# A two-block transformer on one core: second products' weights fetched and split earlier, more first products ahead of the gates, and layer 0's second product turned to sums by feature

## The chip, the cores and the metric

The kernel runs on one core of one Trainium2 chip. The metric is the device time of one execution in microseconds, and of several executions the median is compared. A core has five engines that run their own instruction streams in order and wait for one another by semaphores: TensorE (PE in the profile, with its weight loads as PEld), VectorE (DVE), ScalarE (ACT), GpSimd (POOL) and SyncE (SP). SP, POOL and ACT also issue DMAs.

## The reference, cut to what matters

The program is a block of two attention layers on 256 tokens of 1024 features, and behind it a second block with two layers. Each layer of the second block ends in a feed-forward part that chooses 16 of 16384 experts for each token and each of 8 heads:

```
def peer_ffn(x, w_q, sub_keys, u_emb, v_emb):
    ...
        q = (xc @ w_q).reshape(PEER_CHUNK, PEER_HEADS, 2, PEER_HALF)
        s = jnp.einsum('thid,hikd->thik', q, sub_keys).astype(jnp.float32)
        s1, i1 = lax.top_k(s[:, :, 0], PEER_TOPK)
        s2, i2 = lax.top_k(s[:, :, 1], PEER_TOPK)
        ...
        top_s, pos = lax.top_k(cand, PEER_TOPK)
        eidx = jnp.take_along_axis(cidx, pos, axis=-1)
        gate = jax.nn.softmax(top_s, axis=-1)
        u = u_emb[eidx]
        hid = jax.nn.gelu(jnp.einsum('td,thkd->thk', xc, u))
        wgt = (gate * hid.astype(jnp.float32)).astype(xc.dtype)
        return jnp.einsum('thk,thkd->td', wgt, v_emb[eidx])
```

Layer 0 does this for two sets of 256 tokens (`x` and a context), layer 1 for `x` alone.

## The kernel before, in words

For the tokens of `x` the kernel does not gather the chosen experts. It goes over all 16384 experts in 128 chunks of 128, and multiplies by a gate that is zero where an expert was not chosen. This is `peer`, which runs once in each layer.

For chunk j, `hid(j)` is the **first product**: the chunk's rows of `peer_u` times the tokens, then a gelu. It has two forms. The first `nnat` chunks go in plain float32 (`mm1`, L436, 8 matmuls, each in two records of the profile). The others go as three products of halves (`mm3`, L429 to L431, 24 matmuls): each weight chunk is split into a rounded part `wa` (ACT, L295) and a remainder `wb` (DVE, L297). `wgt(j)` loads four chunks of gates (`gp`, SP, L1629), multiplies the gelu by them (DVE, L1632) and splits the result into `W` (ACT L1634, DVE L1635). `vside(j)` is the **second product**: `W` times the chunk's rows of `peer_v`, summed over all chunks in four PSUM banks. In layer 0 (`NT` is 256) the stationary operand is a piece of `W` for 128 tokens and the chunk of `peer_v` streams by in 512 columns: 12 matmuls, sums by token (L1659 to L1661). In layer 1 (`NT` is `TD`, 224 tokens) a 128 by 128 piece of `peer_v` is stationary and `W` streams by: 24 matmuls of 224 columns, sums by feature (L1651 to L1653). The other 32 tokens of layer 1 are done by gathered rows (`rows_x`), as is the whole context of layer 0 (`rows`, 512 gathered rows of 512 KB, on POOL and DVE).

The first `npre` first products stand ahead of the loop, with their results in `gpre` tiles. `ffn_start` mixes them with two pieces of work: `topk`, the choice of the experts (products with `peer_wq` and the keys on PE, L436 and L1289, then a long run of small DVE instructions, and transposes, L1410), and `gbuild`, which builds the gates (DVE L1576 and L1578, PE L1553, ACT L1557) and writes them to DRAM (`G`, issued from ACT, L1564). `lead` advances a side generator by a rate for each unit of the main one, `par` shares by weights, and `until(pe)` runs `peer` up to its `yield None`. In layer 0, `topk` goes with `lead` at rate `EARLY[0]` after `SOLO` steps of its own, and `gbuild` goes with `par`. In layer 1, `topk` and `gbuild` are one chain and go with `par` against the first products.

Weights come through `WS`: `load` issues 512 KB DMAs on SP in the order of the code, `split` makes `wa` and `wb`, and `get` keeps `depth` loads and `lead` splits ahead. All large tiles share one pool of 42 buffers. The order on PE is that of the code up to the end of layer 0's `ffn_start`; behind that, and on the other engines, a scheduler sets the order when the program is built. While `peer` of layer 0 runs, `along` advances `rows` by `RATE[3]` rows for each unit that it yields.

The main loop of `peer` takes 130 steps, each with `hid(j)` where j is `npre` or more, `wgt(j - 1)` and `vside(j - 2)`.

## Time and profile before

| | us |
|---|---|
| median of 3 runs (3629.66 to 3637.85) | 3633.35 |
| the profiled execution | 3631.59 |
| its span, first to last instruction | 3629.5 |

| engine | busy, share of the span |
|---|---|
| PE | 88% |
| PEld | 80% |
| DVE | 77% |
| ACT | 41% |
| POOL | 26% |

The span is the time from the first to the last instruction. A matmul's duration overlaps its neighbours', so the distance between starts says more than the duration. In layer 0 the first matmul of the second product starts 1519.27 us into the span, in layer 1 at 3010.7; all that is told below of places goes by these times. A number in brackets behind a row is how long the engine stood idle before it, and what ended that.

### The profile page before, as it was taken

The page shows a single profiled execution, that of the slowest core. Times are in us where ns is not written, and L with a number is a line of the kernel's source. Part 1 is how long each engine was busy: PE and PEld are TensorE (multiplying, and loading weights), DVE is VectorE, ACT ScalarE, POOL GpSimd, SP SyncE. Part 2 cuts the span into 40 slices and gives each one's busy share as a digit, 9 for nine tenths or more (in the row PEclk, how much of TensorE's full clock was granted, in tenths as well). Part 3 has the DMA queues.
Part 4 walks back from the last instruction along what each step waited for, and adds up shares of the span by engine and source line. Part 5 has one row for each costly group of instructions (what it writes and reads, how often), then busy time and mean ns, then how long its engine had stood idle before and what let it go on. Part 6 is the DMA issues. An engine that isn't in the chain of part 4 may idle for free. (4 is left out here: it accounts for less than half of the span.)

```text
span 3629.5 us, 60668 instructions
## 1 busy us (share of the span) xinstructions
PE 3205.7 (88%) x23160; PEld 2911.8 (80%) x23160; DVE 2780.5 (77%) x5718; ACT 1484.5 (41%) x2788; POOL 936.3 (26%) x831
## 2 busy tenths in 40 slices
PE   7989999878699788679999999768999689999999
PEld 5877999657598777558888888658888589999999
DVE  4375675877899799899889899797575968777655
ACT  3454444314355203424434344334362154444444
POOL 2002112123234301475555555251000003111000
PEclk9989999988799899789999999879999799999999
DMA  8537457657688937999999999775444099888764
GB/s 308 163 123 281 159 162 266 211 208 261 226 280 314 343 123 226 324 419 393 379 369 383 371 387 390 239 278 185 134 126 171 25 295 350 298 284 289 259 217 151
DMA packets 315427, 941.06 MB, mean 259 GB/s; under 512 B 29616, under 2 KB 93136, under 8 KB 315136
## 3 DMA queue, kind: packets, MB, share of 16 engines
q1 hardware_dynamic: 130848, 468.77, 36.3%
q0 software_dynamic: 118816, 432.76, 33.0%
q10 hardware_dynamic: 65472, 35.66, 3.3%
q8 instruction: 181, 2.97, 0.3%
q14 instruction: 110, 0.90, 0.1%
HBM read 893.01 MB, written 43.02 MB: 258 GB/s over the span
## 5 line engine op out<-in xcount | busy, mean ns | idle before, releaser
L297 DVE TENSOR_TENSOR wb<-wr,wa 128x1024 fp32r<-128x1024 f32 x842 | 1010.3, 1222 | 289.8 <-ACT wa L295 267.2
L295 ACT CAST wa<-wr 128x1024 fp32r<-128x1024 f32 x842 | 852.1, 1046 | 87.2 <-DMA wr<-in_w 27.4
L429 PE MATMUL pu<-hnh,wa 128*128 128x256 f32 x2000 | 585.9, 293 | 23.1 <-ACT wa L295 22.7
L431 PE MATMUL pu<-hnh,wb 128*128 128x256 f32 x2000 | 582.0, 291 | 23.2 <-DVE wb L297 23.0
L430 PE MATMUL pu<-hnl,wa 128*128 128x256 f32 x2000 | 579.3, 290 | 1.6 <-DVE hnl L559 1.6
L1447 POOL DMA_INDIRECT row<-in_pu,ridx x256 | 357.4, 1396 | 516.6 <-DVE wb L297 92.3
L429 PE MATMUL pu<-xh,wa 128*128 128x256 f32 (+1 forms) x1728 | 484.1, 280 | 0.9 <-ACT xh L1618 0.9
L430 PE MATMUL pu<-xl,wa 128*128 128x256 f32 (+1 forms) x1728 | 483.3, 280 | 1.5 <-DVE xl L1619 1.5
L1447 POOL DMA_INDIRECT row<-in_pv,ridx x256 | 362.6, 1417 | 466.4 <-DVE wb L297 113.3
L431 PE MATMUL pu<-xh,wb 128*128 128x256 f32 (+1 forms) x1728 | 482.8, 280 | 0.0
L429 PEld LDWEIGHTS pu<-hnh,wa 128*128 128x128 f32 x2000 | 397.3, 199 | 37.5 <-ACT wa L295 25.7
L431 PEld LDWEIGHTS pu<-hnh,wb 128*128 128x128 f32 x2000 | 396.8, 198 | 30.9 <-DVE wb L297 29.2
L430 PEld LDWEIGHTS pu<-hnl,wa 128*128 128x128 f32 x2000 | 397.3, 199 | 2.6 <-DVE hnl L559 2.1
L429 PEld LDWEIGHTS pu<-xh,wa 128*128 128x128 f32 x1728 | 333.3, 193 | 10.3 <-ACT wa L295 4.3
L430 PEld LDWEIGHTS pu<-xl,wa 128*128 128x128 f32 x1728 | 333.2, 193 | 5.2 <-DVE xl L1619 1.8
L431 PEld LDWEIGHTS pu<-xh,wb 128*128 128x128 f32 x1728 | 332.5, 192 | 1.6 <-issue 0.4
L436 PE MATMUL pu<-xn,wr 128*128 128x256 f32 (+1 forms) x1408 | 325.8, 390 | 4.4 <-ACT xn L573 4.4
L1469 DVE SCALAR_TENSOR_TENSOR racc<-row,rwg,racc 128x1024 f32<-128x1024 f32 x254 | 325.9, 1283 | 0.4
L1459 DVE CUSTOM_DVE_ANT_0 row<-row,xr 128x1024 f32<-128x1024 f32 x256 | 311.0, 1221 | 5.6 <-issue 5.2
L436 PEld LDWEIGHTS pu<-xn,wr 128*128 128x128 f32 x1408 | 276.3, 200 | 44.9 <-issue 7.5
L1609 ACT ACTIVATE gel<-pu 128x256 f32<-128x256 f32 (+1 forms) x204 | 75.7, 371 | 566.6 <-PE pu L431 532.6
L1651 PE MATMUL pm<-W,wa 128*128 128x224 f32 x1024 | 276.0, 275 | 1.6 <-ACT wa L295 1.6
(430 smaller groups left out, 6395.3 us busy)
## 6 DMA issues: line engine op xcount, KB each, us to landing
wr<-in_w SPq DMA_DIRECT2D x288, 512.0 KB
wr<-in_pu SPq DMA_DIRECT2D x256, 512.0 KB
wr<-in_pv SPq DMA_DIRECT2D x256, 512.0 KB
wr<-in_w POOLq DMA_DIRECT2D x130, 512.0 KB
wm<-in_wmod POOLq DMA_DIRECT2D x96, 512.0 KB
G<-gt ACTq DMA_DIRECT2D x60, 512.0 KB
gp<-G SPq DMA_DIRECT2D x32, 512.0 KB
gp<-G SPq DMA_DIRECT2D x32, 448.0 KB
```

Of the source, the lines that this page charges most:

```text
L295: nc.scalar.copy(a, r)
L297: nc.vector.tensor_tensor(b, r, a, op=OP.subtract)
L429: mm(out, ah, bh, start=i == 0, stop=False)
L430: mm(out, ah, bl, start=False, stop=False)
L431: mm(out, al, bh, start=False, stop=i == n - 1)
L436: s.nc.tensor.matmul(out, w[:, k * 128:(k + 1) * 128], x(k), start=k == 0, stop=k == 7)
L1447: nc.gpsimd.indirect_dma_start(out=t, out_offset=None, in_=tab[w], in_offset=bass.IndirectOffsetOnAxis(ap=s.ridx[:, tt, i:i + 1], axis=0))
L1459: v.tensor_tensor_reduce(t, t, xr[tt], 1.0, 0.0, OP.mult, OP.add, hid[:, i:i + 1])
L1469: v.scalar_tensor_tensor(out[tt], t, wg[:, i:i + 1], out[tt], op0=OP.mult, op1=OP.add)
L1609: nc.scalar.activation(g, bank[:, :NT], AF.Gelu_apprx_tanh)
L1651: mm(o, vh[:, c], W[:, 0], start=j == 0 and d % 2 == 0, stop=False, skip_group_check=True)
```

## The change

- `NPRE` goes from (20, 24) and (20, 28) to (20, 28) and (24, 36): layer 0 has 28 first products ahead of the loop, 20 of them plain; layer 1 has 36, 24 of them plain.
- Layer 1's `ffn_start` is now built as layer 0's: `lead` during `topk` (rate 4.0), `par` with `gbuild` (64 to 75). Layer 0's weight in `par` goes from 50 to 60.
- `peer` loads four chunks of `peer_v` and splits two before its `yield None`, that is before the first gates are loaded.
- The second product of layer 0 takes the form of layer 1's, with 256 columns, and its sums by feature are added to `h` in place; the copies (L1690), the transposes and the additions by 128 columns of `add_ffn` (L1532, L1535) are left out for `x`.

```diff
-NPRE = (20, 24), (20, 28)
-
-EARLY = 6.0, 50.0
+NPRE = (20, 28), (24, 36)
+
+EARLY = (6.0, 60.0), (4.0, 75.0)
...
             hid(j)
             yield NT / (75 if j < nnat else 100)
+
+        wv.load(DV + 2)
+        wv.split(2)
         yield None
...
         def vside(j):
             vh, vl = wv.get()
             W = Wt.pop(j)
-            if NT < T:
-                for d in range(8):
...
-                return
-            for tt in range(NT // 128):
-                wh, wl = W[:, 0, tt * 128:(tt + 1) * 128], W[:, 1, tt * 128:(tt + 1) * 128]
-                for dh in range(2):
-                    c, bank = slice(dh * 512, dh * 512 + 512), acc[tt, dh]
-                    mm(bank, wh, vh[:, c], start=j == 0, stop=False)
-                    mm(bank, wh, vl[:, c], start=False, stop=False)
-                    mm(bank, wl, vh[:, c], start=False, stop=j == 127)
+            for d in range(8):
+                c = slice(d * 128, (d + 1) * 128)
+                o = acc[d // 4, d // 2 % 2][:, d % 2 * T:d % 2 * T + NT]
+
+                mm(o, vh[:, c], W[:, 0], start=j == 0 and d % 2 == 0, stop=False, skip_group_check=True)
+                mm(o, vh[:, c], W[:, 1], start=False, stop=False, skip_group_check=True)
+                mm(o, vl[:, c], W[:, 0], start=False, stop=j == 127, skip_group_check=True)
...
         h = s.h_load(s.hd["x"], eng)
+        m5 = s.mod(l, 0, 5)
+        for d in range(8):
+            x = h.ch(d)[:, :NT]
+            v.scalar_tensor_tensor(x, acc[d // 4, d // 2 % 2][:, d % 2 * T:d % 2 * T + NT], m5(d), x,
+                                   op0=OP.mult, op1=OP.add)
         if NT < T:
...
-        for tt in range(2 if NT == T else 0):
-            evs = []
-            for dh in range(2):
-                evs.append(s.s2([128, 512], "pev"))
-                nc.scalar.copy(evs[-1], acc[tt, dh])
-            s.add_ffn(h, l, 0, tt, evs)
...
-    tk = k.topk(l, rx["xn"], ws, eng, rx, skew=bool(early))
+    tk = k.topk(l, rx["xn"], ws, eng, rx, skew=l == 0)
...
-    if not early:
-        gb = lambda: k.gbuild(rx, G, k.nc.scalar, ntc, skew=False)
-        yield from par(k, (chain(tk, gb), TG), (pre, tot))
-        return
     yield from lead(tk, (pre, early))
-    yield from par(k, (k.gbuild(rx, G, k.nc.scalar, ntc), 64.0), (pre, tot))
+    yield from par(k, (k.gbuild(rx, G, k.nc.scalar, ntc, skew=l == 0), 64.0), (pre, tot))
...
-        drain(along(ffn_start(k, 0, rx, ws, k.G[0], pe, *EARLY), rows, RATE[2]))
+        drain(along(ffn_start(k, 0, rx, ws, k.G[0], pe, *EARLY[0]), rows, RATE[2]))
...
-    drain(ffn_start(k, 1, rx, ws, k.G[1], pe, None, NPRE[1][1] * 2.99, ntc=TD // 32))
+    drain(ffn_start(k, 1, rx, ws, k.G[1], pe, *EARLY[1], ntc=TD // 32))
```

Three places show how the instructions move. The first is SP's queue in layer 0, where the first gates `gp` are loaded; `in_pu` and `in_pv` are the tables of the first and the second product. Before:

```order
L282 DMA wr_14648<-in_pu 128x1024
L282 DMA wr_14758<-in_pu 128x1024
L1629 DMA gp_15043<-G_98 128x1024
L282 DMA wr_15059<-in_pv 128x1024
L282 DMA wr_15061<-in_pv 128x1024
L282 DMA wr_15063<-in_pv 128x1024
L282 DMA wr_15097<-in_pv 128x1024
L282 DMA wr_15128<-in_pv 128x1024
L1629 DMA gp_15152<-G_98 128x1024
```

The same place of SP's queue with the change:

```order
L282 DMA wr_15018<-in_pv 128x1024
L282 DMA wr_15020<-in_pv 128x1024
L282 DMA wr_15022<-in_pv 128x1024
L282 DMA wr_15024<-in_pv 128x1024
L1631 DMA gp_15194<-G_98 128x1024
L282 DMA wr_15287<-in_pv 128x1024
L1631 DMA gp_15323<-G_98 128x1024
```

Four of the five chunks of `peer_v` that stood behind the first gates now stand ahead of them, and one is left behind them.

The second place is PE in layer 1, right behind the last products with the keys (L1289) of `topk`, up to the transposes L1410 that wait for the choices; each pair of L436 rows on one `pu` is one first product. Before:

```order
L436 MATMUL pu_27848<-xn_27035,wr_27701 128x224 x3
L436 MATMUL pu_27905<-xn_27034,wr_27734 128x224 x4
L436 MATMUL pu_27905<-xn_27035,wr_27734 128x224 x4
L1410 MATMUL pm_27763<-ct,tt_27764 128x128
L1410 MATMUL pm_27763<-ct,tt_27767 128x128
L1410 MATMUL pm_27763<-ct,tt_27770 128x128
```

The same place on PE with the change:

```order
L436 MATMUL pu_29231<-xn_28532,wr_29198 128x224 x3
L436 MATMUL pu_29250<-xn_28531,wr_29210 128x224 x4
L436 MATMUL pu_29250<-xn_28532,wr_29210 128x224 x4
L436 MATMUL pu_29263<-xn_28531,wr_29229 128x224 x4
L436 MATMUL pu_29263<-xn_28532,wr_29229 128x224 x4
L436 MATMUL pu_29282<-xn_28531,wr_29248 128x224 x4
L436 MATMUL pu_29282<-xn_28532,wr_29248 128x224 x4
L436 MATMUL pu_29337<-xn_28531,wr_29261 128x224 x4
L436 MATMUL pu_29337<-xn_28532,wr_29261 128x224 x4
L436 MATMUL pu_29374<-xn_28531,wr_29280 128x224 x4
L436 MATMUL pu_29374<-xn_28532,wr_29280 128x224 x4
L1410 MATMUL pm_29309<-ct,tt_29310 128x128
```

Five whole first products stand there instead of one, so four more. One more stands between the six transposes and the first gate matmul (L1553), where before there was none.

The third place is PE in layer 0's main loop: one second product, `pm` being the four banks of sums. Before, the whole of it:

```order
L1659 MATMUL pm_15033<-wa_18007,W_18002 128x512
L1660 MATMUL pm_15033<-wb_18008,W_18002 128x512
L1661 MATMUL pm_15033<-wa_18007,W_18002 128x512
L1659 MATMUL pm_15034<-wa_18007,W_18002 128x512
L1660 MATMUL pm_15034<-wb_18008,W_18002 128x512
L1661 MATMUL pm_15034<-wa_18007,W_18002 128x512
L1659 MATMUL pm_15035<-wa_18007,W_18002 128x512
L1660 MATMUL pm_15035<-wb_18008,W_18002 128x512
L1661 MATMUL pm_15035<-wa_18007,W_18002 128x512
L1659 MATMUL pm_15036<-wa_18007,W_18002 128x512
L1660 MATMUL pm_15036<-wb_18008,W_18002 128x512
L1661 MATMUL pm_15036<-wa_18007,W_18002 128x512
```

With the change, the first half of one:

```order
L1652 MATMUL pm_15184<-W_19818,wa_19823 128x256
L1653 MATMUL pm_15184<-W_19818,wa_19823 128x256
L1654 MATMUL pm_15184<-W_19818,wb_19824 128x256
L1652 MATMUL pm_15184<-W_19818,wa_19823 128x256
L1653 MATMUL pm_15184<-W_19818,wa_19823 128x256
L1654 MATMUL pm_15184<-W_19818,wb_19824 128x256
L1652 MATMUL pm_15185<-W_19818,wa_19823 128x256
L1653 MATMUL pm_15185<-W_19818,wa_19823 128x256
L1654 MATMUL pm_15185<-W_19818,wb_19824 128x256
L1652 MATMUL pm_15185<-W_19818,wa_19823 128x256
L1653 MATMUL pm_15185<-W_19818,wa_19823 128x256
L1654 MATMUL pm_15185<-W_19818,wb_19824 128x256
```

It goes on in the same way for the two other banks: 24 matmuls of 256 columns stand for 12 of 512.

## Rows read from the trace of the kernel before

**Rows 1.** Busy time by stretch: us, busy us (instructions), clock share, DMA share, GB/s

```profile
core 0: us, PE busy (x) PEld busy (x) DVE busy (x) ACT busy (x) POOL busy (x), PEclk, DMA share, GB/s
1440.00:1519.00 79.00, 40.96 (x364) 36.68 (x362) 60.73 (x91) 33.54 (x145) 25.62 (x20) 0.71 0.90 285
1519.00:1631.00 112.00, 85.90 (x337) 66.57 (x337) 110.29 (x156) 34.03 (x54) 80.11 (x53) 0.87 1.03 419
1631.00:2272.00 641.00, 594.49 (x3660) 532.85 (x3661) 583.16 (x770) 267.29 (x416) 343.33 (x236) 0.98 0.99 382
2852.00:2885.00 33.00, 1.80 (x6) 1.19 (x7) 31.26 (x169) 4.73 (x14) 0.00 (x0) 0.56 0.00 0
2885.00:2976.00 91.00, 79.46 (x681) 75.59 (x681) 69.61 (x111) 45.88 (x237) 0.00 (x0) 0.88 0.78 240
```

**Rows 2.** The same view for L1660 alone, four to a second product

```profile
1519.00:1631.00 112.00, 42.43 (x96) 20.56 (x96) 0.87 1.03 419
1631.00:2272.00 641.00, 168.45 (x412) 81.35 (x412) 0.98 0.99 382
```

**Rows 3.** Timeline of PE, layer 0's main loop: start, us, instruction [idle before]

```profile
1719.19 0.28 PE L431 MATMUL pu<-xh,wb 128*128 128x256 f32 x1
1719.31 0.40 PE L1659 MATMUL pm<-wa,W 128*128 128x512 f32 x1
1719.54 0.40 PE L1660 MATMUL pm<-wb,W 128*128 128x512 f32 x1
...
1724.93 0.40 PE L1659 MATMUL pm<-wa,W 128*128 128x512 f32 x1
...
1732.41 1.20 PE L1659 MATMUL pm<-wa,W 128*128 128x512 f32 x4 [1.71 <-ACT wa L295]
```

**Rows 4.** Waits by pair: us in total, times, longest

```profile
PE pm L1659 <- ACT wa L295: 85.6, 32, 17.1
```

**Rows 5.** Timeline of ACT ahead of such a wait

```profile
1706.17 0.38 ACT L1609 ACTIVATE gel<-pu 128x256 f32<-128x256 f32 x1 [5.23 <-PE pu L430]
...
1706.74 1.99 ACT L295 CAST wa<-wr 128x1024 fp32r<-128x1024 f32 x2
```

**Rows 6.** Timeline of SP, DVE and PE where layer 0's second products begin

```profile
1506.71 0.33 SPq L1629 DMA_DIRECT2D gp<-G  x1
1507.15 5.35 SPq L282 DMA_DIRECT2D wr<-in_pv  x5
...
1515.40 1.43 DVE L1632 TENSOR_TENSOR gpre<-gpre,gp 128x256 f32<-128x256 f32 x4 [8.09 <-DMA gp<-G]
...
1519.27 2.08 PE L1659 MATMUL pm<-wa,W 128*128 128x512 f32 x4 [17.14 <-ACT wa L295]
```

**Rows 7.** Timeline of PE in layer 1, end of the choices

```profile
2847.64 4.33 PE L436 MATMUL pu<-xn,wr 128*128 128x224 f32 x22
2874.37 0.47 PE L1410 MATMUL pm<-ct,tt 128*128 128x128 f32 x1 [22.41 <-ACT tt L1409]
2881.63 1.33 PE L1410 MATMUL pm<-ct,tt 128*128 128x128 f32 x5 [6.79 <-ACT tt L1409]
2885.38 0.37 PE L1553 MATMUL pm<-gat,hot 128*128 128x128 f16 x2 [2.42 <-DVE gat L1578]
```

**Rows 8.** Timeline of ACT in layer 1's main loop, two steps in a row

```profile
3201.43 0.36 ACT L1609 ACTIVATE gel<-pu 128x224 f32<-128x224 f32 x1 [2.26 <-PE pu L431]
...
3206.79 0.36 ACT L1609 ACTIVATE gel<-pu 128x224 f32<-128x224 f32 x1 [2.27 <-PE pu L431]
```

**Rows 9.** Groups by line, of the page: the remainders of split weights

```profile
L297 DVE TENSOR_TENSOR wb<-wr,wa 128x1024 fp32r<-128x1024 f32 x842 | 1010.3, 1222 | 289.8 <-ACT wa L295 267.2
```

**Rows 10.** End of layer 0's additions (timeline), and a 256-column addition's group

```profile
2276.57 4.23 DVE L1535 SCALAR_TENSOR_TENSOR h<-pu,modT,h 128x128 f32<-128x128 f32 x16
...
L1266 DVE SCALAR_TENSOR_TENSOR h<-pu,modT,h 128x256 f32<-128x256 f32 x24 | 10.6, 480 | 31.8 <-PE pu L431 27.0 <-issue 4.9
```

**Rows 11.** Timeline of SP and DVE in layer 1, the first gates

```profile
2986.19 0.33 SPq L1629 DMA_DIRECT2D gp<-G  x1
...
3004.13 1.29 DVE L1632 TENSOR_TENSOR gpre<-gpre,gp 128x224 f32<-128x224 f32 x4
```

More of the change, by code (lines that the diff above doesn't have):

```diff
@@ L1645, in vside @@
             W = Wt.pop(j)
-            if NT < T:
-                for d in range(8):
-                    c = slice(d * 128, (d + 1) * 128)
-                    o = acc[d // 4, d // 2 % 2][:, d % 2 * T:d % 2 * T + NT]
-                    mm(o, vh[:, c], W[:, 0], start=j == 0 and d % 2 == 0, stop=False, skip_group_check=True)
-                    mm(o, vh[:, c], W[:, 1], start=False, stop=False, skip_group_check=True)
-                    mm(o, vl[:, c], W[:, 0], start=False, stop=j == 127, skip_group_check=True)
-                return
-            for tt in range(NT // 128):
-                wh, wl = W[:, 0, tt * 128:(tt + 1) * 128], W[:, 1, tt * 128:(tt + 1) * 128]
-                for dh in range(2):
-                    c, bank = slice(dh * 512, dh * 512 + 512), acc[tt, dh]
-                    mm(bank, wh, vh[:, c], start=j == 0, stop=False)
-                    mm(bank, wh, vl[:, c], start=False, stop=False)
-                    mm(bank, wl, vh[:, c], start=False, stop=j == 127)
+            for d in range(8):
[4 more added lines that the diff above has]
+                mm(o, vl[:, c], W[:, 0], start=False, stop=j == 127, skip_group_check=True)
         for j in range(130):
@@ L1672, in peer @@
         h = s.h_load(s.hd["x"], eng)
+        m5 = s.mod(l, 0, 5)
[3 more added lines that the diff above has]
+                                   op0=OP.mult, op1=OP.add)
         if NT < T:
             rows = rows()
-            m5 = s.mod(l, 0, 5)
-            for d in range(8):
-                x = h.ch(d)[:, :NT]
-                v.scalar_tensor_tensor(x, acc[d // 4, d // 2 % 2][:, d % 2 * T:d % 2 * T + NT], m5(d), x,
-                                       op0=OP.mult, op1=OP.add)
             bank = s.ps("u")
```

## The prediction

> **What bounds the kernel now.** I read the busy time by stretch first, to see which engine is full where the change falls, then the timelines of PE and of its releasers at four places. Layer 0's feed-forward part has two regimes [rows 1, 2]. From 1519 to 1631 us 96 records of L1660 make 24 second products, almost all without a first product beside them: 112.0 / 24 = 4.67 us a step. DVE is busy for 110.3 of the 112 us and PE for 85.9, so DVE (with the gathered rows of the context) and the DMAs (share 1.03) set the pace. From 1631 to 2272 there are 412 / 4 = 103 steps of 641 / 103 = 6.22 us, with a first product in nearly all. PE is busy for 594.5 of 641 us there, DVE for 583.2: PE is the bound, with waits. The reader is to see in [rows 3] what a step is made of. Matmuls of 256 columns start 0.12 us apart, matmuls of 512 columns 0.23, and two second products in a row start 1724.93 - 1719.31 = 5.62 apart, PE full. But at 1732.41 PE stood for 1.71 us until ACT had rounded a weight chunk. Without the first of them such waits are 31, of 68.5 us in total [rows 4]. ACT is not slow there, it is in line: its gelu waited for the first product to end, and the rounding stands behind the gelu [rows 5]. At 1502 PE fell idle for 17.14 us, up to the first second product [rows 6].
>
> In layer 1 PE is full in the main loop: ACT's gelu waits for PE at each step, and the steps are 3206.79 - 3201.43 = 5.36 us long [rows 8], 48 matmuls of 0.112 us, so 2.68 for a first and 2.68 for a second product. What PE loses there it loses at the end of the choices: between 2851.97 and 2885.38 it waits 22.41 + 6.79 + 2.42 = 31.6 us for DVE's selection and what hangs on it [rows 7], with DVE busy for 31.3 of 33 us and no DMA running [rows 1].
>
> **The change part by part.** The sum is made against the profiled execution's 3631.59 us (span 3629.5 and 2.1 around it); it stands 1.76 below the median of the runs, 3633.35.
>
> *Layer 0's second product turned.* 12 matmuls of 512 columns go, 24 of 256 come. The new form takes 24 x 0.12 = 2.88 us. The old one took 5.62 - 2.88 = 2.74, the first product beside it being 24 matmuls of 256 columns too [rows 3]. That is 0.14 us more a step. In the 100 steps with a first product PE is the bound and it counts: +14. The wait for ACT does not shrink, for it hangs on the end of the first product and not on the second. In the 28 steps without one, DVE covers it; if that cover is gone it costs 28 x 0.14 = 4 more. From the other side, PE's waits (641 - 594.5 = 46.5 us) could take all of it in, and then it costs nothing. Bounds 0 to +18; I take +14, the rows being from the same loop.
>
> [...]
>
> *Four more first products beside layer 0's gates.* Four steps go at 4.67 instead of 6.22: -6.2. Their four remainders on DVE, 1.22 us each [rows 9], now fall into the building of the gates: 4.9 us, where DVE idled 79 - 60.7 = 18.3 us between 1440 and 1519 [rows 1]. Half of it hides, I say: +2.5. Together -3.7, with bounds of -6.2 (all hidden) and -1.3 (none).
>
> *Weights of the second product ahead of the gates, layer 0.* Before, the first gates were issued at 1506.71 and multiplied at 1515.40, while five chunks of `peer_v` were issued right behind them on the same queue; PE began at 1519.27, when the first chunk was rounded [rows 6]. Now four chunks are loaded and two split by then. From the multiplication to PE were 3.9 us. The multiplication, the rounding and the remainder of W stay in that path, some 1.5 us by the 0.36 us of one multiplication [rows 6]: -2.4. The gates' flight of 8.7 us no longer shares the engines with five chunks: between 0 and 5 x 0.524 MB at 419 GB/s [rows 1] = -6.3, and I take -2, since row gathers stay in flight. Together -4.4, bounds -8.7 and 0. What is late next is the gates themselves, which neither edit hastens. SP's queue has nothing else behind the four loads but the gates' load, and that waits for G anyway.
>
> *End of layer 0.* Four copies, 16 transposes and 16 additions of 128 columns go; the additions alone took 4.23 us [rows 10]. Eight additions of 0.48 come, straight from the banks, the first ones before the last bank is complete. The additions alone give 4.23 - 8 x 0.48 = -0.4; if they hide altogether, -4.2. I take -3.
>
> Layer 0: +14 - 3.7 - 4.4 - 3 = +2.9.
>
> *Layer 1's first products into the choices.* The order shows five more of them ahead of the first gate matmul, four before the transposes and one behind. One is 16 records at 4.33 / 22 = 0.197 us [rows 7], 3.15 us; five fill 15.7 of the 31.6 idle us. In all eight more stand ahead of the loop, four of them plain, 4 x 3.15 + 4 x 2.68 = 23.3 us. So 23.3 - 15.7 = 7.6 us are left over for the building of the gates, where PE had 91 - 79.5 = 11.5 us idle [rows 1]. I let 3 of these take some in. The loop is shorter by 8 x 2.68 = -21.4. Sum -21.4 + 7.6 - 3 = -16.8. Bounds: all the idle used, -25.3; none of it, and the gates late by what was pushed ahead of them, -8.
>
> Behind these first products on PE wait the gate matmuls, then ACT's evictions, the write of G and the load of the first gates. That load was issued at 2986.19 and multiplied at 3004.13 [rows 11], 6.6 us ahead of the first second product at 3010.7. So a delay of the gates up to about 6 us is free, as long as PE has first products to do; beyond it the gain is eaten. The loads and splits of `peer_v` ahead of the gates I cost at nothing here: PE is on first products then. Without that cover they are two remainders of 1.22, 2.4 us.
>
> Total: +2.9 - 16.8 = -13.9. Profiled execution 3617.7; median 3633.35 - 13.9 = 3619.5, and I forecast **3620**, in its own range of 3610 to 3630.
>
> **The rivals.** *The turned product costs nothing*: PE's waits for ACT take in the 0.14 us of each step, or the short form follows closer than now. For it: 46.5 us of waits. Against: the wait begins at the end of a first product, so a longer second product does not eat it, and 0.12 us is measured in this very loop. -13.9 - 14 = -27.9: 3605. Chance 0.15. [...]
>
> *The gates come late.* In layer 1, PE runs more first products between the tables, so G is complete later than PE is free, and the second products wait. For it: 17.9 us from the issue of the first gates to their use, with the DMAs busy. Against: in the changed build's order PE has some six first products behind the last table. Layer 1 then gives the bound of -8, and in layer 0 too the fetch of weights gains only half: -13.9 + 8.8 + 2.2 = -2.9: 3630. Chance 0.22.
>
> *Buffers, slower.* All large tiles share 42 buffers. In layer 0 four chunks of `peer_v`, two of them split, hold two raw and four split tiles through the end of the gates, and a seventh tile of first products one more. Row gathers on POOL then wait for buffers, and DVE, which in that stage idled 18.3 of 79 us, idles as long again. The rows left undone are done in the stretch where DVE is full (110.3 of 112). Price: +18.3, and the two gains of 3.7 and 4.4 are lost: +26.4. -13.9 + 26.4 = +12.5: 3646. For it: DMA share 0.90 and POOL with little done in that stage. Against: the six tiles are held for the last part of the stage only. It decides from 21 us on. Chance 0.11.
>
> **How the numbers follow.** Forecast 0.52, turned product free 0.15, gates late 0.22, buffers 0.11. The range of 3604 to 3638 leaves out the lower part of the second case and most of the last one. 0.2% is 7.3 us, about what a measurement here can tell from no change. Faster than 3626.1: 0.47 of the forecast's 0.52, all of the 0.15, 0.05 of gates late, 0.67. Slower than 3640.6: 0.09, from the last case. The rest, 0.24, is within.
>
> **What would show it.** Right: starts of the turned product 0.12 us apart and 5.76 between full steps in layer 0; the 1.71 us wait every fourth step still there; PE's idle at the transposes of layer 1 down from 31.6 to some 16 us; the first second product of layer 1 some 5 us later than before relative to the start of the choices, and the loop behind it 21 us shorter. Wrong: a wait of PE for `W` or for the gates ahead of either loop that is longer than before; DVE idle between the gates of layer 0 with POOL waiting; or steps in layer 0's loop that keep their 6.22 us.

## The result and the profile after

The changed kernel is slower: 3656.40 us median of 4 runs (3653.97 to 3660.76), where the kernel before took 3634.61 on the same chip (3629.66 to 3637.85). The ratio is 1.0068, 95% interval 1.0053 to 1.0084. The forecast was 3620, its range ended at 3638.

The profiled execution took 3660.76 us, with a span of 3658.9 against 3629.5. The starts of marker instructions in PE's timeline cut this difference into stretches. "Gates" runs from the first to the last gate matmul (L1553), "to V" from there to the first second product, "loop" from the first to the last matmul of the second products.

| us | before | after | difference | forecast |
|---|---|---|---|---|
| up to layer 0's first gate matmul | 1383.1 | 1388.8 | +5.7 | 0 |
| layer 0, gates | 118.8 | 156.0 | +37.2 | +2.5 |
| layer 0, to V | 17.4 | 17.3 | -0.1 | -4.4 |
| layer 0, loop | 755.6 | 752.0 | -3.6 | +7.8 |
| from there to layer 1's transposes (L1410) | 599.5 | 600.0 | +0.5 | -3 |
| layer 1, L1410 to first second product | 136.3 | 147.6 | +11.3 | +4.6 |
| layer 1, loop | 611.2 | 589.7 | -21.5 | -21.4 |

One profile is one execution: stretches that no edit touched differ by several us between kernels (the first line; the stretch to layer 1's transposes was 584 to 601 us in the kernels below). The stretch from L1410 to layer 1's first second product was 129.8 to 132.8 us in the three kernels below that leave layer 1 and G as they were, so the 136.3 of the kernel before is on the high side. Only the larger differences are read from such stretches.

The loss is one line: the building of layer 0's gates. Busy time by stretch for that stage up to the first second product, before and after (us, busy us and instructions of PE, PEld, DVE, ACT, POOL, clock share, DMA share, GB/s):

```profile
1383.00:1520.00 137.00, 92.22 (x780) 81.15 (x778) 117.88 (x179) 59.59 (x282) 40.57 (x33) 0.81 0.90 288
```

```profile
1389.00:1562.00 173.00, 108.25 (x871) 96.70 (x868) 124.91 (x182) 65.53 (x291) 45.06 (x35) 0.78 0.82 261
```

DVE got 7.0 us of work more and PE 16.0, but the stage grew by 36. No engine is full in it now: DVE idles 48 us where it idled 19. Between the first and the last gate matmul alone, before and after:

```profile
1383.10:1501.90 118.80, 91.16 (x777) 80.48 (x775) 111.64 (x165) 55.38 (x268) 33.48 (x26) 0.85 0.88 278
```

```profile
1388.80:1544.80 156.00, 108.17 (x873) 96.89 (x871) 120.85 (x174) 63.01 (x278) 40.19 (x31) 0.81 0.79 251
```

While the gates were built, DVE was nearly full before the change: it idled 118.8 - 111.6 = 7.2 us. Of the 37.2 us that the building grew by, 9.2 are more work of DVE and 28.0 more idle time of DVE. The waits by pair say for whom (us in total, times, longest), before and after:

```profile
ACT gt L1557 <- DMA G<-gt: 7.0, 1, 7.0
...
DVE wb L297 <- ACT wa L295: 7.9, 3, 5.5
```

```profile
DVE wb L297 <- ACT wa L295: 31.7, 8, 8.9
ACT gt L1557 <- DMA G<-gt: 30.3, 4, 9.9
...
PE pm L1553 <- DVE gat L1578: 23.2, 17, 5.6
```

One instance in the timelines of ACT, DVE and PE shows how the three hang together (start, us, instruction, idle before it and its releaser):

```profile
1473.70 0.37 ACTq L1564 DMA_DIRECT2D G<-gt  x1
...
1474.16 7.23 ACTq L1564 DMA_DIRECT2D G<-gt  x3
1481.44 0.79 ACT L1557 ACTIVATE gt<-pm 128x128 f32<-128x128 f32 x4 [7.26 <-DMA G<-gt]
1482.08 1.07 ACT L295 CAST wa<-wr 128x1024 fp32r<-128x1024 f32 x1
```

```profile
1474.86 1.28 DVE L1578 TENSOR_TENSOR gat<-hot,id 128x1024 f16<-128x1024 f16 x2
1483.18 1.23 DVE L297 TENSOR_TENSOR wb<-wr,wa 128x1024 fp32r<-128x1024 f32 x1 [7.03 <-ACT wa L295]
1484.32 1.29 DVE L1576 TENSOR_TENSOR hot<-io,id 128x1024 f16<-128x1024 f16 x2
```

```profile
1476.58 1.55 PE L1553 MATMUL pm<-gat,hot 128*128 128x128 f16 x24
1483.20 0.58 PE L429 MATMUL pu<-xh,wa 128*128 128x256 f32 x1 [5.07 <-ACT wa L295]
```

At 1474.16 ACT's queue issues three writes of G, and the issue holds it for 7.23 us. Behind them stands the rounding L295 of a weight chunk of a split first product. DVE's next instruction is that chunk's remainder L297, and behind it stand the operands of the next tables (`hot`, `gat`). All three engines stand for some 5 to 7 us. The first of the four writes takes 0.37 us, and those behind it are longer; this is the line of all 32 writes of this stage (durations in ns, shortest, median, longest):

```profile
L1564 ACTq DMA_DIRECT2D G<-gt x32: 366/1257/7045, 1400.6 to 1552.7; - x32
```

All of them move the same bytes in equally many runs, so the length of a hold is not a fixed price of a write; what the later ones wait for isn't shown.

Before, with four split first products at the end of the stage, DVE stood 3 times for a rounding; now 8 times.

Where layer 0's second products begin, the timelines of SP, DVE and PE answer to [rows 6]:

```profile
1555.49 0.33 SPq L1631 DMA_DIRECT2D gp<-G  x1
...
1561.12 1.43 DVE L1634 TENSOR_TENSOR gpre<-gpre,gp 128x256 f32<-128x256 f32 x4 [4.19 <-DMA gp<-G]
...
1562.04 1.22 PE L1652 MATMUL pm<-W,wa 128*128 128x256 f32 x4 [16.96 <-ACT W L1636]
```

The load and the multiplication are quicker, 6.6 us from issue to first second product where it was 12.6, but the load is issued 10.7 us behind the last table where it was 4.9: ACT's last writes of G take their issue time here too. PE's wait is 17 us as before, for W and no longer for a weight.

The turned product in layer 0's main loop behaves as its term said; starts of matmuls where the two products change (answers to [rows 3]):

```profile
1771.58 0.39 PE L1652 MATMUL pm<-W,wa 128*128 128x256 f32 x1 [1.71 <-ACT wa L295]
...
1777.49 0.28 PE L1652 MATMUL pm<-W,wa 128*128 128x256 f32 x1
1777.61 0.28 PE L1653 MATMUL pm<-W,wa 128*128 128x256 f32 x1
...
1783.25 0.28 PE L1652 MATMUL pm<-W,wa 128*128 128x256 f32 x1
```

Starts are 0.12 us apart, a full step is 1783.25 - 1777.49 = 5.76, and the wait of 1.71 is still there. By stretch (all instructions, then L1654 alone, eight records to a second product; answers to [rows 1, 2]):

```profile
1562.00:1682.00 120.00, 98.52 (x675) 95.83 (x676) 119.93 (x172) 35.94 (x57) 78.66 (x60) 0.83 1.00 402
1682.00:2314.00 632.00, 585.58 (x4776) 580.25 (x4774) 572.07 (x756) 258.35 (x404) 320.03 (x230) 0.99 0.98 379
```

```profile
1562.00:1682.00 120.00, 58.04 (x217) 42.83 (x217) 0.83 1.00 402
1682.00:2314.00 632.00, 219.45 (x808) 151.33 (x808) 0.99 0.98 379
```

Some 27 steps without a first product at 120 / 27.1 = 4.42 us, DVE full; then 632 / 101 = 6.26 us a step, 0.04 more than before. The additions at the end come from the banks, eight in two groups (DVE's timeline, answers to [rows 10]):

```profile
2313.65 1.65 DVE L1669 SCALAR_TENSOR_TENSOR h<-pm,modT,h 128x256 f32<-128x256 f32 x4
...
2316.41 1.65 DVE L1669 SCALAR_TENSOR_TENSOR h<-pm,modT,h 128x256 f32<-128x256 f32 x4
```

They last from 2313.65 to 2318.06, 4.4 us with a row's work between, as long as the sixteen did.

In layer 1, at the end of the choices, PE now waits less, as forecast (answers to [rows 7] and [rows 11]; timelines of PE and SP):

```profile
2914.02 0.47 PE L1410 MATMUL pm<-ct,tt 128*128 128x128 f32 x1 [8.62 <-ACT tt L1409]
2921.28 1.33 PE L1410 MATMUL pm<-ct,tt 128*128 128x128 f32 x5 [6.79 <-ACT tt L1409]
...
2927.28 1.19 PE L1553 MATMUL pm<-gat,hot 128*128 128x128 f16 x18
```

```profile
3051.70 0.33 SPq L1631 DMA_DIRECT2D gp<-G  x1
```

8.62 + 6.79 = 15.4 us are left of 31.6.

Over the whole program, the page's line of the remainders (answers to [rows 9]) has DVE's idle time ahead of them up from 289.8 to 324.4 us, nearly all of it waits for a rounding:

```profile
L297 DVE TENSOR_TENSOR wb<-wr,wa 128x1024 fp32r<-128x1024 f32 x838 | 1005.3, 1222 | 324.4 <-ACT wa L295 307.4
```

### The profile page after: what moved, and what is told of

The parts are those of the page before. It is cut to its first block, busy times and chain, and to the rows that moved or that the text cites. A ratio compares the mean times of both kernels' runs of the same rounds, so it can differ in the third digit from the quotient of the medians.

```text
span 3658.9 us, 63647 instructions
## 1 busy us (share of the span) xinstructions
PE 3233.3 (88%) x24648; PEld 3013.9 (82%) x24648; DVE 2774.0 (76%) x5706; ACT 1478.5 (40%) x2780; POOL 918.4 (25%) x831
## 4 chain that ended last, share of the span: by engine, by line
PE 44%; DVE 8%; issue 3%; ACT 2%; ACTq 1%; DMA 1%; POOL 0%; DVEq 0%; POOLq 0%; SPq 0%
PE pu L431 7%; PE pu L429 7%; PE pu L430 7%; PE pm L1652 6%; PE pm L1654 5%; PE pm L1653 5%; PE pu L436 2%; DVE racc L1469 1%; DVE wb L297 1%; ACT wa L295 1%; ACTq L1564 1%; DVE row L1459 1%; PE pm L1553 1%; PE pm L1045 0%; DMA row<-in_pv,ridx 0%
## 5 line engine op out<-in xcount | busy, mean ns | idle before, releaser
L297 DVE TENSOR_TENSOR wb<-wr,wa 128x1024 fp32r<-128x1024 f32 x838 | 1005.3, 1222 | 324.4 <-ACT wa L295 307.4
L295 ACT CAST wa<-wr 128x1024 fp32r<-128x1024 f32 x838 | 849.2, 1047 | 85.2 <-DMA wr<-in_w 26.7
L1652 PE MATMUL pm<-W,wa 128*128 128x256 f32 (+1 forms) x2048 | 571.0, 285 | 84.1 <-ACT wa L295 63.5
L429 PE MATMUL pu<-hnh,wa 128*128 128x256 f32 x2000 | 589.7, 295 | 25.0 <-ACT wa L295 24.3
L1653 PE MATMUL pm<-W,wa 128*128 128x256 f32 (+1 forms) x2048 | 569.3, 284 | 0.0
L1654 PE MATMUL pm<-W,wb 128*128 128x256 f32 (+1 forms) x2048 | 544.9, 284 | 3.1 <-DVE wb L297 3.1
L1447 POOL DMA_INDIRECT row<-in_pu,ridx x256 | 348.2, 1360 | 529.1 <-DVE wb L297 103.0
L1652 PEld LDWEIGHTS pm<-W,wa 128*128 128x128 f32 x2048 | 399.7, 196 | 90.8 <-ACT wa L295 69.4
L431 PEld LDWEIGHTS pu<-hnh,wb 128*128 128x128 f32 x2000 | 400.3, 200 | 28.4 <-DVE wb L297 26.5
L1653 PEld LDWEIGHTS pm<-W,wa 128*128 128x128 f32 x2048 | 401.3, 197 | 0.1
L1654 PEld LDWEIGHTS pm<-W,wb 128*128 128x128 f32 x2048 | 384.9, 196 | 5.2 <-DVE wb L297 5.0
L429 PEld LDWEIGHTS pu<-xh,wa 128*128 128x128 f32 x1696 | 331.2, 195 | 23.7 <-ACT wa L295 17.4
L436 PE MATMUL pu<-xn,wr 128*128 128x256 f32 (+1 forms) x1472 | 334.9, 386 | 4.3 <-ACT xn L573 4.3
```

The source lines that it names most:

```text
L295: nc.scalar.copy(a, r)
L297: nc.vector.tensor_tensor(b, r, a, op=OP.subtract)
L429: mm(out, ah, bh, start=i == 0, stop=False)
L431: mm(out, al, bh, start=False, stop=i == n - 1)
L436: s.nc.tensor.matmul(out, w[:, k * 128:(k + 1) * 128], x(k), start=k == 0, stop=k == 7)
L1447: nc.gpsimd.indirect_dma_start(out=t, out_offset=None, in_=tab[w], in_offset=bass.IndirectOffsetOnAxis(ap=s.ridx[:, tt, i:i + 1], axis=0))
```

## The experiments

The theories at the start. 1: split first products among the gates tie DVE's queue to ACT's, which the issue of G's writes holds. 2: the tiles that the change holds earlier leave too few of the 42 buffers. 3: the turned product costs. 4 (the count itself) and 5 (another way) came up on the way. Ratios are to the kernel before on the same chip, with 95% intervals.

**Layer 0 with 24 first products again.**

```diff
-NPRE = (20, 28), (24, 36)
-EARLY = (6.0, 60.0), (4.0, 75.0)
+NPRE = (20, 24), (24, 36)
+EARLY = (6.0, 50.0), (4.0, 75.0)
```

> The changed kernel with layer 0's 24 first products beside the choices, as before (20 plain, 4 split, rate 50), all else as changed. Theory 1 (a split first product among the gates ties DVE to ACT's queue, where the writes of G are issued; DVE's remainder stands ahead of the tables' operands): the stage of layer 0's gates falls back from 156 to about 119 us between its first and last gate matmul, and the time to about 3624 us: 3634 before, -10 for layer 1, +3 for the turned product in the loop, -2 at the end of layer 0, 0 to -3 for the weights ahead. Theory 2 (the chunks of the second product's weights, loaded and split early, hold buffers that the gathers and loads need): the stage stays at 140 us or more, 3645. Theory 3 (the turned product costs): the stage is back, but the loop is longer by 14 or more: 3638 or above.

Measured 1.0009 (0.9996 to 1.0023), 3635.76 against 3632.49. Gates 132.2 us, loop 762.3. Most of the loss is gone, but the stage is still 13 us longer than before. That fitted neither theory's number. With the turned product alone the stage takes 118.7 us (below), so the difference speaks for the early weights.

**No early weights in layer 0.**

```diff
-        wv.load(DV + 2)
-        wv.split(2)
+        if l == 1:
+            wv.load(DV + 2)
+            wv.split(2)
```

> The changed kernel without the early load and split of the second product's weights in layer 0; layer 1 keeps them. Theory 1: the gate stage stays at some 156 us, and the time within 5 us of the changed kernel's 3656, 3654 to 3661. Theory 2 (these six tiles are what the gathers and loads lack): the gate stage falls by 25 us or more, and the time to 3630 or below. Theory 3: 3656.

Measured 1.0043 (1.0029 to 1.0057), 3649.67. Gates 152.1. Theory 2's number did not come. By the middles of the two ratios (1.0068 and 1.0043) the early weights cost some 9 us here, instead of giving 4.4; the intervals overlap by a little, so this pair alone does not show it.

**The turned product alone, in the kernel before.**

```diff
             vh, vl = wv.get()
             W = Wt.pop(j)
-            if NT < T:
-                for d in range(8):
+            for d in range(8):
...
```

> The kernel before with one part of the change: layer 0's second product and its end by feature, layer 1 and the choices as before. Theories 1 and 2: the loop's full steps are 0.14 us longer, partly given back by fewer waits, +3 as between the two traces, and -2 at the end: 3636 against 3634. Theory 3 (the turned product is what made the change slower): 3648 or more; my forecast's own terms give 3634 + 14 - 3 = 3645.

Measured 1.0022 (1.0008 to 1.0036), 3640.18: +7.7. Gates 118.7 as before, loop 765.6 where it was 755.6, and the stretch behind it 599.9, so the new end gives nothing. Theory 3 explains about a third of the net loss; with -3 for the end my terms give 11, inside the interval (+3 to +13).

**27 of the 28 plain.**

```diff
-NPRE = (20, 28), (24, 36)
+NPRE = (27, 28), (24, 36)
```

> The changed kernel with 27 plain and 1 split of layer 0's 28 first products beside the choices: as many of them, as many tiles of results and early chunks of the second product's weights as in the changed kernel, but only one split weight and the split of the input at the very end. Theory 1 (each rounding on ACT and remainder on DVE among the gates ties DVE's queue to ACT's, where the writes of G are issued): the gate stage is 120 to 130 us instead of 156, the time 3618 to 3632. Theory 2, now with a wider cause (the split input, two tiles more than the plain one, and three tiles for each weight in splitting, leave too few of the 42 buffers for tables, gathers and loads): the same, for both go. Theory 4 (28 first products are simply more work than PE can place there): the stage stays at 145 or more, 3645 or above.

Measured 0.9966 (0.9952 to 0.9980), 3617.92 against 3630.09. Gates 123.3. DVE's waits for a rounding are down to two (up to the first second product):

```profile
DVE wb L297 <- ACT wa L295: 6.3, 2, 4.6
```

As many first products fit, if they aren't split. One of the 28 stays split since the code makes the halves of the input, which the loop needs, at the first split one. Theory 4 falls. Theories 1 and 2 both expected this.

**G written from SP's queue.**

```diff
-k.gbuild(rx, G, k.nc.scalar, ntc, skew=l == 0)
+k.gbuild(rx, G, k.nc.sync, ntc, skew=l == 0)
```

> The changed kernel with the writes of G issued from SP's queue instead of ACT's. Theory 1: ACT is never held by an issue, DVE's waits for a rounding fall from 31.7 us to some 6, and the gate stage from 156 us to 135 or less; time 3630 to 3640, unless the loads of first products' weights, which stand behind the writes on SP then, are late in turn. Theory 2 (buffers): the tiles of G are released by the writes as late as now; stage 150 or more, time 3650 or more.

Measured 1.0081 (1.0055 to 1.0108), 3661.19. Gates 146.1. The exception in the expectation is what happened. SP's timeline shows the writes there with the weight loads behind them; the waits of DVE follow:

```profile
1468.47 6.23 SPq L1564 DMA_DIRECT2D G<-gt  x4
1474.81 2.90 SPq L282 DMA_DIRECT2D wr<-in_pu  x3
```

```profile
DVE wb L297 <- ACT wa L295: 24.9, 5, 11.6
```

The hold went along with the writes: now a rounding is late since its weight is. Layer 1 lost too: from L1410 to the first second product it took 163.0 us, against 147.6 in the changed kernel. The Trainium skill, "DMA: Bandwidth & Descriptors", section "Issuing engines are not separate DMA queues", says that issuing from several engines saves only the sequencer's issue time, "which is usually small relative to the DMA itself". The first half agrees as far as this run goes: ACT lost the issue time and SP took it on. In this stage, though, the issue is not small beside the DMA:

```profile
L1564 SPq DMA_DIRECT2D G<-gt x32: 359/1016/3367, 1398.3 to 1536.4; - x32
...
G<-gt SPq DMA_DIRECT2D x60, 512.0 KB, 4.9
```

The issue of a write takes 1.0 us in the median and up to 3.4, where the median from issue to landing is 4.9 (second line, from the profile's page, all 60 writes), and four in a row hold SP's queue for 3 to 7 us. This run doesn't decide between the theories.

**Four more split, in the kernel before.**

```diff
-NPRE = (20, 24), (20, 28)
+NPRE = (16, 24), (20, 28)
```

> The kernel before with 16 plain and 8 split first products beside layer 0's choices instead of 20 and 4: the count stays 24, four more are split. Theories 1 and 2: the gate stage grows from 119 us by 20 to 35, the time to 3652 to 3668. Theory 4 (the count): 3634, within 5.

Measured 1.0037 (1.0023 to 1.0050), 3641.45 against 3630.09. Gates 127.8, to V 22.0. With the count unchanged four splits cost 11 us, about half of what was expected, so theory 4 falls a second time. The dose is smaller than in the changed kernel.

**38 buffers in the kernel before.**

```diff
-BUFS = dict(pg=42)
+BUFS = dict(pg=38)
```

> The kernel before with 38 buffers for large tiles instead of 42, everywhere; only the stage of layer 0's gates is judged. Theory 2 (buffers): four tiles are about what the earlier split of the input (two) and one weight in splitting (two) hold, so the gate stage stretches by 20 us or more from 119. Theory 1 (ACT's queue): 5 us or less, since the split first products stand where they stood.

Measured 0.9991 (0.9976 to 1.0006). Gates 123.2. Four tiles less cost 4 us in this stage and nothing in all, so theory 2 lacks its size. The changed kernel holds up to seven tiles more, which this run alone does not cover; but there the early weights' tiles cost 4 us of the stage (156.0 against 152.1), and further below two more tiles in use go with a shorter stage. With these three theory 2 falls as the main cause.

**Layer 1's part alone, in the kernel before.**

```diff
-NPRE = (20, 24), (20, 28)
-EARLY = 6.0, 50.0
+NPRE = (20, 24), (24, 36)
+EARLY = (6.0, 50.0), (4.0, 75.0)
...
```

> The kernel before with only layer 1's part of the change: 24 plain and 36 first products in all, started beside the choices at rate 4 and then 75, the operands of the next table made one step ahead no longer in layer 1. No early weights of the second product. My forecast's term for layer 1 gives -16.8, so 3617 where the kernel before takes 3634. The traces of the changed kernel give -10, so 3624, since in its gate stage PE was full and the gates of layer 1 came 11 us later.

Measured 0.9968 (0.9950 to 0.9985), 3618.76 against 3632.01: -13, interval -18 to -5. My term of -16.8 lies inside. From L1410 to the first second product it took 147.9 us, as in the changed kernel. (The expectation names an edit that there isn't: in layer 1 the tables' operands are made ahead in neither kernel.)

**G laid out by block of tokens.**

```diff
-s.G = [s.dr.tile([32, 128, 8, 4, 32], F32, ...
+s.G = [s.dr.tile([4, 8, 128, 1024], F32, ...
-eng.dma_start(G[jq * 8:(jq + 1) * 8, :, tc].rearrange("g p j t -> p g (j t)"),
-              gt[jq].rearrange("p (g j) t -> p g (j t)", g=8))
+eng.dma_start(G[jq, tc], gt[jq].rearrange("p j t -> p (j t)"))
```

> The changed kernel with G laid out by block of 32 tokens, so that a write of G is 128 runs of 4 KB instead of 1024 of 512 B, and a read of four gates 1024 runs of 512 B instead of 128 of 4 KB; all results the same. Theory 1 (ACT is held by the issue of G's writes, three of which take 6 to 10 us, and the roundings of split first products stand behind them, DVE's remainders behind those, and the gates' operands behind these): the issue takes under 2 us for four, DVE's waits for a rounding fall from 31.7 us to 12 or less, the gate stage of layer 0 from 156 to 135 us or less, the time to 3640 or below, unless the loop pays for its reads. Theory 5 (the split first products delay the gates by another way, such as the time of weights to land or the order of PE): the stage stays at 145 us or more.

Measured 0.9993 (0.9977 to 1.0009), 3630.29 against 3632.01: by this alone the time is back at that of the kernel before. Not all of that is the change's loss, for the same edit shortens the kernel before as well (below). Gates 136.5, loop 754.9. ACT's issue at the same place, and DVE's waits:

```profile
1463.90 3.90 ACTq L1564 DMA_DIRECT2D G<-gt  x3
...
1488.51 2.73 ACTq L1564 DMA_DIRECT2D G<-gt  x3
```

```profile
DVE wb L297 <- ACT wa L295: 15.7, 6, 4.1
```

Three writes hold the queue for 2.2 to 3.9 us instead of 4.2 to 9.8, and the waits halved. The stage came out just above the 135 us that theory 1 expected, the issue and the waits further above its 2 and 12 us. Bytes are the same, the runs are longer and fewer. The Trainium skill, "Perfetto Trace Analysis", section "DMA Instruction — HWDGE (DVE, Sync)", has the issuing sequencer's time contain the generation of descriptors, and engines start before it ends if they are more than the buffer holds. Fewer runs with a shorter issue agree with that; but a first write of 1024 runs took 0.37 us, so the number of runs alone does not make the hold.

**Plain, with the old second product in layer 0.**

```diff
-            for d in range(8):
+            if NT < T:
+                for d in range(8):
...
```

> The changed kernel with 27 plain and 1 split first products in layer 0, and layer 0's second product and its end as before. If the turned product costs what the kernel with it alone showed (7.7 us by the medians, 10 in the loop by its profile), this is 8 to 10 us under the kernel with plain first products and the turned product: ratio to before 0.9940, 3608 to 3611 where the kernel before takes 3630. If the turned product costs nothing, 3618.

Measured 0.9924 (0.9898 to 0.9950), 3605.67. The loop is 746.4 where the turned product had 757.1: 10.7 us, the same as in the kernel before (10.0).

**The same without early weights in layer 0.** The edit is that of the second run.

> As the last one, and without the early load and split of the second product's weights in layer 0, so that there DVE and ACT have two roundings and two remainders less among the gates. If each split among the gates costs some 6 us through ACT's queue (the four of the dose cost 11 to 14, the two early ones 5 to 9), this is 5 us or more under the last one, 3605 or less. If the early weights give what my forecast said (-4.4), it is 4 above it.

Measured 0.9920 (0.9888 to 0.9952), 3605.34: no difference shows, with intervals of 9 to 12 us to either side. Gates 123.4 and to V 19.3, against 121.4 and 18.4. By the profiles early weights do not cost here, when first products are plain; a few us either way stay open.

**That kernel with G by block.**

> The last kernel (27 plain and 1 split in layer 0, old second product, no early weights in layer 0, layer 1 as changed) with G laid out by block of 32 tokens, as in the run that shortened the issue of G's writes. Theory 1: with hardly a split first product among layer 0's gates nothing on DVE hangs on ACT's queue there, so the shorter issue gives 5 us or less in layer 0's gate stage (123 us), where it gave 19.5 in the changed kernel; layer 1, whose split first products do stand among the gates, keeps its gain of some 4 us (147.6 to 143.6 in the changed kernel). 3600, ratio to before 0.9905 to 0.9925. If the layout shortens the stage by itself, because the tables' evictions wait behind the writes with any first products, it is 15 us or more there and the ratio 0.988 or less.

Measured 0.9892 (0.9872 to 0.9912), 3593.82 against 3634.36. Gates 113.4: 10 us less, between the two expectations. The tables' evictions stand behind the writes as well, so a shorter issue gives something without splits, and about twice as much (19.5) with them.

**Rounding one first product earlier, in the changed kernel.**

```diff
             nc.scalar.copy(a, r)
-            with s.k.behind():
-                nc.vector.tensor_tensor(b, r, a, op=OP.subtract)
-            s.sp[s.ns] = (a, b)
+            s.pend.append((s.ns, r, a, b))
             s.ns += 1
+        while s.pend and s.pend[0][0] < (to - 1 if s.late and to < s.n else to):
+            i, r, a, b = s.pend.pop(0)
+            with s.k.behind():
+                nc.vector.tensor_tensor(b, r, a, op=OP.subtract)
+            s.sp[i] = (a, b)
...
-wu = WS(..., depth=DU, lead=LU, ...
+wu = WS(..., depth=DU + (l == 0), lead=LU + (l == 0), ...
```

> The changed kernel with one edit in the split of layer 0's first-product weights: a chunk is loaded and rounded on ACT one first product earlier, and its remainder on DVE is issued as late as now, one first product behind its rounding; in the main loop too. All else as in the changed kernel, two more tiles in use. If DVE stands for a rounding because the remainder follows it at once (the second half of theory 1), its waits for ACT's rounding in the gate stage fall from 31.7 us to 10 or less, and the stage from 156 to 140 or less, as much as the shorter issue of G's writes gave (136.5). If the splits stretch the gates through PE or through DVE's added work (7 remainders more, 8.6 us), the stage stays at 150 or more even though the waits go.

Measured 1.0008 (0.9996 to 1.0019), 3633.69 against 3629.24. Gates 142.8. The waits fell less than expected (the remainder's line is L301 in these two kernels):

```profile
DVE wb L301 <- ACT wa L295: 19.2, 5, 9.9
```

The longest of them, 9.9 us, ends with a rounding that stood behind four writes, issued from 1431.19 to 1438.79: one first product of lead was not enough there.

**The same with G by block.**

> The same edit in the kernel with G laid out by block of 32 tokens (stage 136.5 us, DVE's waits for a rounding 15.7). If these waits are what is left of the stretch, the stage comes to 125 or less. If the rest is DVE's added work and PE's order, it stays at 132 or more.

Measured 0.9954 (0.9936 to 0.9972), 3615.08. Gates 122.5. One short wait is left, and DVE is busy for 122.2 of 140 us up to the first second product:

```profile
DVE wb L301 <- ACT wa L295: 2.6, 1, 2.6
```

```profile
1388.00:1528.00 140.00, 99.82 (x876) 90.63 (x874) 122.24 (x178) 66.76 (x291) 48.28 (x35) 0.84 0.87 321
```

**G by block in the kernel before.**

> The kernel before with G laid out by block of 32 tokens, nothing else. If ACT's hold by the writes costs only through split first products, of which five stand at the end of that stage, the stage of layer 0's gates stays within 5 us of 119 and the time within 7 of the kernel before. If the tables' evictions, which stand behind the writes too, lose by it, as the last run let it look (10 us of 123), the stage falls to 112 or less and the time by 8 us or more.

Measured 0.9956 (0.9939 to 0.9972), 3615.68 against 3629.24. The time fell by 13.6 as the second expectation said, the stage to 113.7, a little less than it said. While the gates are built DVE is now full:

```profile
1385.40:1499.10 113.70, 91.49 (x777) 80.86 (x775) 111.56 (x165) 57.50 (x274) 32.84 (x27) 0.85 0.82 295
```

In the profile layer 1 has the larger part: L1410 to the first second product 120.2 us against 136.3, or against 129.8 to 132.8 in the other kernels with that layer unchanged. This run is the fair base for the changed kernel with the same layout (0.9993): by the middles of the ratios the change still costs 0.4% there. Its layer-1 part gains nothing in these two profiles: stretch and loop together take 120.2 + 611.2 = 731.4 us here and 143.6 + 589.7 = 733.3 there.

**The fastest, with earlier rounding in both layers.**

> The fastest kernel so far (27 plain and 1 split first products in layer 0, second product as before there, no early weights in layer 0, layer 1 as changed, G by block of 32 tokens) with first-product weights rounded one first product earlier and their remainders issued as late as now, in both layers. If layer 1's gates too are held by DVE standing for a rounding (39.6 us of such waits in the changed kernel, one of 24.3), the time from its transposes to its first second product falls from 141.3 to 137 or less and the whole by 4 us or more: ratio to before 0.988 or less. If these waits lie beside PE's work there, since PE is full in that stage, nothing moves: 0.9885 to 0.990.

Measured 0.9877 (0.9861 to 0.9894), 3591.23 against 3638.43. L1410 to the first second product is 132.9 us where it was 141.3. DVE's waits ahead of a remainder there and PE's wait for `gat` fell (the kernel of the run with G by block, then this one):

```profile
DVE wb L297 <- ACT wa L295: 27.0, 7, 17.2
DVE wb L297 <- ACT gpre L1607: 9.2, 2, 4.7
PE pm L1553 <- DVE gat L1577: 5.0, 1, 5.0
```

```profile
DVE wb L301 <- ACT wa L295: 27.1, 9, 10.7
PE pm L1556 <- DVE gat L1580: 0.8, 1, 0.8
```

That speaks for the same tie in layer 1, but the stretch differs by 6.5 us between kernels that are alike there, so one pair doesn't show it. The two ratios' intervals overlap, so for the whole time this edit's gain isn't shown. It is the fastest version measured: 1.2% under the kernel before.

## Why the prediction was wrong

**The step that failed** is "Four more first products beside layer 0's gates", -3.7 with bounds of -6.2 and -1.3. I counted the remainders as 4.9 us of work against 18.3 us of DVE's idle time, and let half of it hide. Two things were wrong. Of the 18.3 us, 17 - 5.3 = 11.7 lie behind the last table, and 8.1 of these are the wait for the first gates [rows 6]:

```profile
1502.00:1519.00 17.00, 0.13 (x2) 0.00 (x0) 5.28 (x12) 3.89 (x17) 7.09 (x7) 0.50 1.01 350
```

While the gates were built DVE idled only 7.2 us in 118.8, so there was hardly room, and its added work came to 9.2 us: six remainders more instead of four, two of them those of the early weights, and one more row of the context. And work was the smaller part of the cost: DVE's idle time grew by 28.0 us. Queues run in order, so a remainder that is not ready stops everything behind it, and what is behind it here are the operands of the tables. Why a rounding is late stood in the trace of the kernel before, in ACT's timeline, in a line that I did not look at since issuing isn't counted as busy:

```profile
1406.18 7.98 ACTq L1564 DMA_DIRECT2D G<-gt  x3
```

The bounds were those of the work, so the range didn't hold the result either. With the order that lets rounding lead and with the shorter issue, the stage of 156.0 us becomes 142.8 and 136.5, and with both 122.5. The shorter issue takes 5.1 us off the stage of the kernel before too (118.8 to 113.7). So with the short issue in both the change costs 136.5 - 113.7 = 22.8 us in that stage, and with the earlier rounding in the changed kernel as well 122.5 - 113.7 = 8.8, about as much as DVE's added work. 28.4 of the 37.2 us are thus gone with the two edits; that the last 8.8 are DVE's work is argued from its busy time (118.1 of the 122.5 us) and not tried.

```profile
1388.20:1510.70 122.50, 99.30 (x874) 90.47 (x873) 118.07 (x171) 65.43 (x284) 43.04 (x30) 0.89 0.85 315
```

**Weights ahead of the gates**, -4.4, bound 0 above: nothing in the time to the first second product, and, with split first products around them, perhaps a cost: 9 us by the middles of the two ratios, 5 by the medians, with intervals that overlap. I said that the gates themselves would be late next, and that is so. But I left the two roundings and remainders of these chunks out of the gates' stage; with 24 first products the stage takes 132.2 us with them (first run) and 118.7 without (turned product alone), and DVE's waits for a rounding 16.9 against 6.1. With 28 split as in the change they make 3.9 us (156.0 against 152.1), with 27 plain nothing, so what they cost depends on what stands around them.

**The turned product**, +14: right in kind and somewhat too large. 0.12 us and 5.76 a step as said. +10.0 and +10.7 in the loops of two pairs, +7.7 by medians; loops with the old product and 24 first products ahead take 751.2 to 757.9 us over five kernels, so a pair is good to some 5 us. PE's waits took in a little: 85.6 us of waiting for a weight before [rows 4], 81.1 with the turned product alone. The rival that it costs nothing is out.

**The loop by the four first products fewer**, -6.2: -9.2 from 755.6 to 746.4 with the old product. **The end**, -3: the additions take as long as before, and no gain shows in that stretch.

**Layer 1**, -16.8: -10.2 by the profiles (-4 to -7 against the kernels with 129.8 to 132.8), -13 by its own run, and nothing by the profiles with G by block in both. The idle time at the transposes fell to 15.4 as said, and the loop by 21.5 as said. In the stage of the gates I let 3 us of PE's idle time be filled. There came a wait of PE for `gat` of 9.6 us instead, behind DVE's wait of 24.3 for a rounding: the same tie. DVE stood there before as well, 34.3 us in all and 17.0 at the longest, now 39.6. The lower bound of -25.3 was wrong as a sum: only 7.6 us were left over to be taken in, so it could not go below -21.4.

**The rivals.** Slower had a chance of 0.09, in a case of buffers at 3646. Its signs came true (POOL waiting, DVE idle between the gates), its mechanism did not: with 38 buffers the stage moves by 4 us, and its price too came from the 18.3 us. "The gates come late" named the right place, but gave as cause PE's load behind the tables, and 3630.

**What stays open.** Why the dose of four splits in the kernel before costs 11 us in all and 9 in the stage, where 20 to 35 were expected there; why the second to fourth write of G hold a queue so much longer than the first; what the layer-1 part is worth when the issue is short; and the stretch from layer 0's end to layer 1's transposes, which varies from 584 to 601 us over kernels that do not differ there.

## What to carry to other kernels

Before work is put into a stage's idle time, look at what each added instruction waits for and at what stands behind it on its engine: an idle share says how much work fits only if that work is ready when its turn comes. Cut the stage where its last instruction ends: idle time behind it takes in nothing. Look at the queue's own rows for DMA issues on an engine that computes too, since they hold it and count as idle. Where one engine makes what another uses, and the first can be held, set them further apart: one first product of lead took 13 us off this stage, and holds of 7.6 us were still longer.

## What the runs showed of the hardware

The issue of a DMA can hold an engine's queue for long: in the stage of layer 0's gates three writes of 0.5 MB in runs of 512 B took 4.2 to 9.8 us of ACT's queue (changed kernel), in runs of 4 KB 2.2 to 3.9, with the same bytes. The write ahead of these three took 0.37 us in the one and 0.33 in the other. Moved to SP, four such writes held that queue for 3 to 7 us. Reading G in the shorter runs instead cost nothing that the loop shows: 754.9 us against 752.0, within what untouched stretches differ by.
